# Hybrid decoder trunk: operands of the products in one aligned pool, slice-major first tiles, and the extra columns as 64-column float32 products

## The chip, the cores and the metric

The kernel runs on one NeuronCore of a Trainium2 chip. Its time is the device time of one execution in microseconds (us), and the median of three executions is compared. "PE" is the matrix engine (PEld its weight loads), DVE, ACT and POOL are the vector, scalar and GpSimd engines, and SP issues the transfers. A change of about 0.2% is what a measurement of this kernel can tell from none.

## The reference

Two layers over 512 tokens of width 1024, all in float32:

```python
for l in range(DEPTH):
    h = rms_norm(x, attn_norm[l])
    proj = h @ w_in[l]            # gates, MLA columns, RWKV columns, conv columns
    o_a = mla_branch(...) @ mla_w_o[l]
    o_b, v_first = rwkv7_branch(...)      # a scan over time, in 8 chunks of 64 in the kernel
    o_b = o_b @ rwkv_w_o[l]
    o_c = short_conv_branch(conv_cols, conv_w[l]) @ conv_w_o[l]
    merged = g[:, :, 0] * o_a + g[:, :, 1] * o_b + g[:, :, 2] * o_c
    x = x + merged @ w_out[l]
    h2 = rms_norm(x, mlp_norm[l])
    x = x + jnp.square(jax.nn.relu(h2 @ w_up[l])) @ w_down[l]
```

The "extra columns" are 32 columns of `w_in` (the shared rotary key) and, in the second layer, 32 columns of `rwkv_v1`. They are needed as one tile of 64 rows, `ext`.

## The kernel before, in words

Activations lie feature-major: 128 features on the partitions, 512 tokens along a row, 8 such slices for the width. A large product is made with three products of a reduced float32 type (fp32r): each operand is split into `hi` and a remainder `lo`, and hi·hi, hi·lo and lo·hi are added up in PSUM (`gemm_steps`, lines 269, 271 and 273). An output tile of 128 features over 8 slices is thus 24 products of 128x512. The weights stream in blocks of 512 columns: a transfer into `raw`, a cast by ACT into `hi` (line 243) and a subtraction by DVE into `lo` (line 244), in the order in which `_blocks` packs them. `xg` holds the split, gain-scaled input; its norm `rstd` is multiplied in when a tile leaves PSUM.

PE's order is the order in which the code is written. The work of a layer is: the first tiles (RWKV columns and the extra columns), the RWKV stage with its chains of small float32 products, attention, the merge of the three branches with `w_out`, and the MLP in four quarters (8 tiles up, 8 tiles down). The generator `independent` (`others`) yields the products that nothing waits for, and `fill(n)` puts n of them between small products that have to wait; the table `FC` holds the n of each place. DVE, ACT, POOL and SP instructions are ordered by the compiler's scheduler, each engine's queue then runs in order.

Places that the change touches:

- Start of a layer: five tiles one after the other (`rwkv_gemm` for "g", "g", "a", "b", "a"); the fourth (layer 0) is the extra columns, padded with zeros to 128. Tile by tile, the first needs all 8 slices of `xg` before it is finished.
- The am stage (lines 668 to 717): DVE and ACT make `ar` and `bk`, and PE multiplies them at line 714 after `fill(FC["am"])`, for j = 0 and 1.
- `chunk_inputs` (lines 840 to 843): 8 products of 64x64, four in one quarter of the array, then four in the other.
- The merge (lines 1164 to 1176): for each m a spilled `z` is read back, multiplied with the branch, added to `mg[m]` (line 1170) and split into `ar` (line 1174) and `mix` (line 1175).
- Tile buffers: one SBUF pool `sb`, which lays its tags out one behind the other in the order of their first use. In `prep` a buffer is 520 words (2080 bytes of a partition) and in `mg` 514 words (2056 bytes), so that their buffers start at many different places of a 2048-byte raster. In the built program `hi`, `lo` and `xg` lie below 79 KB, and start at byte 1120 of the raster; `mix` starts at 640 and `ar` at 672, both above 140 KB; `prep` starts at 1120, 1152, 1184 and so on, `mg` at 672, 704, 736 and so on.

Of the kernel before, what the change touches and what calls it, by code (L numbers as in the profile page):

```python
# [32 lines left out]
C = 64  # L33
# [7 lines left out]
FC = {"ss": 9, "pk": 16, "am": 42, "tri0": 6, "tri1": 10, "join0": 22, "join1": 9, "join2": 8, "in1": 9, "py": 2,  # L41
# [16 lines left out]
def _blocks(inp, l):  # L58
# [3 lines left out]
    for t in RW_ORDER[:3]:  # L62
        out.append(_cols(w_in[:, r0 + t * P:r0 + (t + 1) * P]))
    ex = np.zeros((D, P), w_in.dtype)
    ex[:, 0:32] = w_in[:, a0 + 640:a0 + 672]
    if l > 0:
        ex[:, 32:64] = inp["rwkv_v1"][l - 1]
    out.append(_cols(ex))
    for t in RW_ORDER[3:]:
        out.append(_cols(w_in[:, r0 + t * P:r0 + (t + 1) * P]))  # L70
# [96 lines left out]
def trunk(tc, w, wkv, wq, xin, pos, pp, sm, rg, out, sizes):  # L167
# [4 lines left out]
    const = es.enter_context(tc.tile_pool(name="const", bufs=1))  # L172
    sb = es.enter_context(tc.tile_pool(name="sb", bufs=1))
# [4 lines left out]
    BUFS = {"xg": 16, "mix": 8, "prep": 10, "am": 1, "ar": 4, "inv": 9, "tok": 2, "raw": 3, "hl": 4, "z": 2,  # L178
            "mg": 11, "col": 7, "g": 2, "a": 2, "b": 2, "c": 2}
# [66 lines left out]

    def load_kq(src):
# [4 lines left out]
        hi = tl("prep", (P, 520), F32R)[:, 0:n]  # L252
        lo = tl("kql", (P, WW), F32R, bufs=4)[:, 0:n]
# [33 lines left out]
    def split(tag, src, scale=None, tag_lo=None):  # L287
# [10 lines left out]
        return hi, lo  # L298

# [126 lines left out]
    def rounded(dst, src):  # L426
        ti = tl("prep", (P, 520), I32)[:, 0:NR]
# [64 lines left out]
    for l in range(NL):  # L492
        pr, dv, rgl = ppt[l], drv[l], rgt[l]
        sl = tl("sm", (P, 3 * RW), bufs=1)
        nc.sync.dma_start(out=sl, in_=sm[l])
# [30 lines left out]
        pgs = []  # L526
        at = 2 if l else 3
# [8 lines left out]
        V.tensor_tensor(out=ext[0:64, 1:T + 1], in0=pgs[0][0:64], in1=rstd[0:64], op=ALU.mult)  # L536
        rwkv_cols(RW_ORDER[3], pgs[1])
        for t in RW_ORDER[4:]:
# [24 lines left out]
        def independent():  # L563
# [6 lines left out]
            for j in range(2):  # L570
                cols = []
                for _ in range(3):
                    pg = pt("g")
                    yield from gemm_steps(pg, None, xg)
                    cols.append(evacuated(pg, tl("mg", (P, T + 2))[:, 0:T]))
                    if len(cols) == 2:
                        u = tl("mg", (P, T + 2))
# [89 lines left out]
        for j in range(2):  # L667
# [5 lines left out]
            V.tensor_scalar(out=k2, in0=a_, scalar1=dv[:, 6 + j:7 + j], scalar2=dv[:, 8 + j:9 + j],  # L673
                            op0=ALU.mult, op1=ALU.add)
            V.tensor_tensor(out=k2, in0=k2, in1=kt[j], op=ALU.mult)
            V.tensor_scalar(out=a_, in0=a_, scalar1=-0.5, scalar2=-0.5, op0=ALU.mult, op1=ALU.add)
            eW = tl("prep", (P, 8, C + 1))
# [4 lines left out]
            V.tensor_copy(eC[:, j, :], eW[:, :, C])  # L682

            ex = tl("prep").rearrange("p (b h c) -> p b h c", b=NB, h=2)
            V.tensor_copy(ex, rs16v[:, :, j, :].unsqueeze(3).to_broadcast([P, NB, 2, C]))
# [20 lines left out]
            fill(FC["am"])  # L706
# [115 lines left out]
        def chunk_inputs(b):  # L822
# [17 lines left out]
            for p in range(2):  # L840
                for h, hs in enumerate(hss):
# [43 lines left out]
        def code_split(t):  # L885

            gcol = pcol("kva", t) if t < 2 else pcol("qa", t - 2)
            hi = tl("prep", (P, 520), F32R)[:, 0:T]
# [357 lines left out]
```

## Time and profile before

| | |
|---|---|
| runs shown | 1633.64, 1634.8, 1635.77 us; median 1634.8 |
| profiled execution | 1636.34 us |
| its span, first to last instruction | 1634.6 us |
| granted PE clock, mean | 0.998 |
| busy | PE 99%, PE weight loads 80%, DVE 62%, ACT 40%, POOL 11% |
| products (PE instructions) | 8126 |

How to read it: a product's row shows its duration from first word in to last word out, about 390 ns, but the next product starts while it drains. The distance from start to start, not the duration, is what a product costs the queue of PE; so the busy share of PE is high even where it is slowed. A float32 product that isn't a transpose appears as two records. In a windows view a row is: stretch, its length, busy time and count for each engine asked for, granted PE clock, share of the transfer engines, GB/s. In a timeline a row is start, duration, engine, line, operation, and in brackets the idle time before it with what ended it.

### The profile page before, as it was taken

Reading aid. Unit: us, or ns where it says so; the run is one execution under the profiler, and the core shown is the slowest. Engines: PE = TensorE matmul, PEld = TensorE weight load, DVE = VectorE, ACT = ScalarE, POOL = GpSimd, SP = SyncE. Lnnn points to the kernel's source line nnn. Section 1 sums busy time; section 2 is a strip of 40 time slices with the busy share of each in tenths; the row PEclk is TensorE's granted clock in tenths of the full one; section 3 lists DMA queues with packets and bytes.
Section 4 is the critical chain, followed back from the end, with each engine's and each line's share of the span. In section 5 each row is a group of like instructions: output and inputs, shape, how many; then the busy total and the mean of one; then the engine's idle time right before and its main releaser. Section 6 shows DMA issues by size and latency. Waiting matters only on the chain.

```text
span 1634.6 us, 22593 instructions
## 1 busy us (share of the span) xinstructions
PE 1617.3 (99%) x8126; PEld 1306.0 (80%) x8126; DVE 1016.8 (62%) x1988; ACT 659.3 (40%) x1457; POOL 185.8 (11%) x192
## 2 busy tenths in 40 slices
PE   8999999999999999999999999999999999999998
PEld 7878778877788888888887887887777888888887
DVE  7789577676754444544567886686766544444453
ACT  5332556454443232424333335654534433323241
POOL 1212024102100000000022121251120000000000
PEclk9999999999999999999999999999999999999999
DMA  5323322214323333333432243222143333333333
GB/s 163 95 73 108 110 66 80 82 46 129 123 91 97 97 97 95 95 95 97 141 98 78 79 127 92 63 72 73 51 146 113 92 95 97 97 97 96 93 96 103
DMA packets 85072, 156.79 MB, mean 96 GB/s; under 512 B 10080, under 2 KB 12384, under 8 KB 84448
## 3 DMA queue, kind: packets, MB, share of 16 engines
q1 hardware_dynamic: 84960, 155.35, 32.3%
q8 instruction: 64, 1.05, 0.3%
q14 instruction: 48, 0.39, 0.1%
HBM read 146.40 MB, written 8.91 MB: 95 GB/s over the span
## 4 chain that ended last, share of the span: by engine, by line
PE 93%; DVE 3%; DMA 2%; issue 1%; ACT 0%; SPq 0%; POOL 0%; DVEq 0%; ACTq 0%
PE pg L271 15%; PE pg L269 15%; PE pg L273 15%; PE pa L273 4%; PE pa L271 4%; PE pa L269 4%; PE pb L273 4%; PE pb L271 4%; PE pb L269 4%; PE pc L271 4%; PE pc L273 4%; PE pc L269 4%; PE pa L1115 2%; DMA z<-z_spill 1%; PE pc L1141 1%; DVE lo L244 1%
## 5 line engine op out<-in xcount | busy, mean ns | idle before, releaser
L243 ACT CAST hi<-raw 128x512 fp32r<-128x512 f32 (+1 forms) x499 | 307.1, 618 | 629.2 <-PE pg L271 255.6
L244 DVE TENSOR_TENSOR lo<-raw,hi 128x512 fp32r<-128x512 f32 (+1 forms) x499 | 358.2, 718 | 244.6 <-ACT hi L243 239.1
L269 PE MATMUL pg<-xg,hi 128*128 128x512 f32 x784 | 312.3, 398 | 2.9 <-ACT xg L296 2.2
L271 PE MATMUL pg<-xg,hi 128*128 128x512 f32 x784 | 313.8, 400 | 0.3 <-DVE xg L297 0.3
L273 PE MATMUL pg<-xg,lo 128*128 128x512 f32 x784 | 310.0, 395 | 0.0
L269 PEld LDWEIGHTS pg<-xg,hi 128*128 128x128 f32 x784 | 147.9, 189 | 39.3 <-issue 4.7
L271 PEld LDWEIGHTS pg<-xg,hi 128*128 128x128 f32 x784 | 148.0, 189 | 34.2 <-issue 5.8
L273 PEld LDWEIGHTS pg<-xg,lo 128*128 128x128 f32 x784 | 147.8, 189 | 31.6 <-issue 2.3
L303 POOL TENSOR_TENSOR t<-t,mhalf 128x4 f32<-128x4 f32 (+1 forms) x26 | 48.9, 1882 | 560.8 <-DVE t L314 536.7
L269 PE MATMUL pg<-ar,hi 128*128 128x512 f32 x192 | 75.7, 394 | 0.1
L273 PE MATMUL pg<-ar,lo 128*128 128x512 f32 x192 | 75.5, 393 | 0.0
L273 PE MATMUL pa<-xg,lo 128*128 128x512 f32 x160 | 62.6, 391 | 0.0
L269 PE MATMUL pa<-xg,hi 128*128 128x512 f32 x160 | 62.3, 390 | 0.0
L271 PE MATMUL pa<-xg,hi 128*128 128x512 f32 x160 | 62.3, 389 | 0.0
L271 PE MATMUL pg<-mix,hi 128*128 128x512 f32 x144 | 57.5, 399 | 1.3 <-DVE mix L1175 1.3
L273 PE MATMUL pb<-xg,lo 128*128 128x512 f32 x144 | 56.2, 390 | 0.0
L269 PE MATMUL pb<-xg,hi 128*128 128x512 f32 x144 | 56.1, 390 | 0.0
L271 PE MATMUL pb<-xg,hi 128*128 128x512 f32 x144 | 56.0, 389 | 0.0
L1119 ACT ACTIVATE inv<-pa,t 128x128 f32<-128x128 f32 (+3 forms) x64 | 33.7, 527 | 46.2 <-DVE t L1117 45.7
L271 PE MATMUL pg<-prep,hi 128*128 128x512 f32 x128 | 50.5, 394 | 0.0
L269 PE MATMUL pc<-xg,hi 128*128 128x512 f32 x128 | 50.0, 390 | 0.0
L273 PE MATMUL pc<-xg,lo 128*128 128x512 f32 x128 | 49.8, 389 | 0.0
(385 smaller groups left out, 3197.7 us busy)
## 6 DMA issues: line engine op xcount, KB each, us to landing
raw<-in_w_dram SPq DMA_DIRECT2D x493, 256.0 KB, 2.6
z_spill<-z SPq DMA_DIRECT2D x16, 256.0 KB, 3.1
z<-z_spill SPq DMA_DIRECT2D x16, 256.0 KB, 2.9
raw<-in_wq_dram SPq DMA_DIRECT2D x12, 192.0 KB, 2.3
am<-in_x_dram SPq DMA_DIRECT2D x8, 256.0 KB, 6.1
raw<-in_wkv_dram SPq DMA_DIRECT2D x8, 256.0 KB, 2.7
am<-in_x_dram SPq DMA_DIRECT2D x2, 1024.0 KB, 6.1
x_spill<-am SPq DMA_DIRECT2D x8, 256.0 KB, 2.9
```

Source lines behind the costliest of these rows:

```text
L243: A.copy(hi[:, c], raw[:, c])
L244: V.tensor_tensor(out=lo[:, c], in0=raw[:, c], in1=hi[:, c], op=ALU.subtract)
L269: mm(dst, hi[:, c0:c0 + P], ah, start=(k == 0), stop=False)
L271: mm(dst, hi[:, c0:c0 + P], al, start=False, stop=False)
L273: mm(dst, lo[:, c0:c0 + P], ah, start=False, stop=(k == n - 1))
L303: G.tensor_tensor(out=y, in0=v, in1=mhalf.to_broadcast([P, n]), op=ALU.pow)
L1115: mm(psc[:, 0:n], qT[hf][h // 2][0:HD, h % 2, b * P:n], kT[hf][h // 2][0:HD, h % 2, 0:n], start=True, stop=False)
L1119: A.activation(out=pe[:, 0:n], in_=psc[:, 0:n], func=AF.Exp, bias=nm[:, h:h + 1], accum_out=rsum[:, h:h + 1])
L1141: mm(po[halves[i], f], Vm[hf][kb // 2][:, kb % 2, 2 * f + i], pT[2 * f + i][:, kb * P:(kb + 1) * P], start=(kb == 0), stop=(kb == b))
```

## The change

- A second pool `sbl` is laid out before `sb` and takes `hi`, `lo`, `xg`, `prep`, `mix`, `ar` and `mg`. `prep` and `mg` lose their padding (the padded `eW` and `u` go to `kql`, 520 words). In the built program every buffer of the seven tags now starts at byte 1120 of the 2048-byte raster, between 7 KB and 129 KB (the last buffer of `mg` ends at 132,192 bytes). `raw` gets a fourth buffer.
- The first four tiles are made slice by slice: for each of the 8 slices one weight block holds the 128 columns of all four tiles, and 12 products follow, 3 into each of four PSUM banks. `pack` orders the weights so, and the first transfers alternate between x and weight blocks.
- The extra columns leave the fp32r path: their weights are 64 columns wide, multiplied by the gains on DVE (`weights_by`), and 8 plain float32 products of 64 columns go alternately into the lower and upper half of one PSUM tile; the halves are added after an ACT copy.
- In the am stage two DVE operations, a DVE copy and a small copy per j go to ACT; the fill is 50 for j = 0 and 40 for j = 1 (42 for both before).
- `chunk_inputs` alternates between the two quarters of the array.
- In the merge `z` comes into `inv` (9 buffers; `z` has 2), and the split is written through `places`; the last two are scheduled with priority. The MLP's splits use `places` too.

```diff
-FC = {... "am": 42, ...
+FC = {... "am": (50, 40), ...
...
+    for k in range(KD):
+        out.append(np.concatenate([f[k * P:(k + 1) * P] for f in first], axis=1))
     out.append(_cols(ex))
-    for t in RW_ORDER[3:]:
+    for t in RW_ORDER[4:]:
...
+    sbl = es.enter_context(tc.tile_pool(name="sbl", bufs=1))
     sb = es.enter_context(tc.tile_pool(name="sb", bufs=1))
...
-        if tag in ("prep", "mg") and tuple(shape) == (P, T):
-            return sb.tile([P, 520 if tag == "prep" else T + 2], dt, tag=tag, name=f"{tag}_{cnt[0]}", bufs=BUFS[tag])[:, 0:T]
-        return sb.tile(list(shape), dt, tag=tag, name=f"{tag}_{cnt[0]}", bufs=bufs or BUFS[tag])
+        pool = sbl if tag in ("hi", "lo", "xg", "prep", "mix", "ar", "mg") else sb
+        return pool.tile(list(shape), dt, tag=tag, name=f"{tag}_{cnt[0]}", bufs=bufs or BUFS[tag])
...
+    def weights_by(gains):
+
+        i, off = wpos
+        wpos[0], wpos[1] = i + 1, off + WW * P
+        raw = tl("raw", (P, WW))
+        nc.sync.dma_start(out=raw, in_=w[off:off + WW * P].rearrange("(p n) -> p n", p=P))
+        wx = tl("inv").rearrange("p (k n) -> p k n", n=C)
+        V.tensor_tensor(out=wx, in0=raw.rearrange("p (k n) -> p k n", n=C), in1=gains.unsqueeze(2).to_broadcast([P, KD, C]),
+                        op=ALU.mult)
+        return wx
...
+    def places(m, tag):
+
+        if tag is None:
+            return tuple(tl("mix" if m < 4 else "prep", (P, T), F32R) for _ in range(2))
+        if m < 4:
+            both = tl("ar", (P, 2, T), F32R)
+            return both[:, 0], both[:, 1]
+        return tuple(tl(tag, (P, T), F32R) for _ in range(2))
...
-        if k in (0, 3):
-            ahead.append(load_weights(2))
-    ahead += [load_weights(2), load_weights()]
+        if k < 4:
+            ahead.append(load_weights(2 if k < 2 else 1))
...
-        for i, pst in enumerate(("g", "g", "a", "b", "a")):
-            pgs.append(rwkv_gemm(pst, normed_steps if i == at else None))
-            if i == at:
+        pgs = [pt(pst) for pst in ("g", "g", "a", "b")]
+        for k, (ah, al) in enumerate(xg):
+            hi, lo = weights()
+            for t, pg in enumerate(pgs):
+                c = slice(t * P, (t + 1) * P)
+                mm(pg, hi[:, c], ah, start=(k == 0), stop=False)
+                mm(pg, hi[:, c], al, start=False, stop=False)
+                mm(pg, lo[:, c], ah, start=False, stop=(k == KD - 1))
+        for _ in normed_steps:
+            pass
...
+        wx = weights_by(pr[:, PC["attn"]:PC["attn"] + 8])
+        pe = pt("a")
+        for k in range(KD):
+            i = k % 2
+            mm(pe[halves[i]], wx[:, k], xt[:, k], start=(k < 2), stop=(k >= KD - 2))
+        pgs.append(pt("b"))
+        for i, _ in enumerate(gemm_steps(pgs[4], None, xg)):
+            if i == 8:
                 normed_spread()
...
+        odd = tl("inv")
+        A.copy(odd[0:64], pe[64:128])
...
-            V.tensor_scalar(out=k2, in0=a_, scalar1=dv[:, 6 + j:7 + j], scalar2=dv[:, 8 + j:9 + j],
-                            op0=ALU.mult, op1=ALU.add)
+            A.activation(out=k2, in_=a_, func=AF.Identity, scale=dv[:, 6 + j:7 + j], bias=dv[:, 8 + j:9 + j])
...
-            for p in range(2):
-                for h, hs in enumerate(hss):
+            for h, hs in enumerate(hss):
+                for p in range(2):
                     mm(prs[p][halves[1 - p], hs], AM[halves[p], h, b, p, halves[1 - p]], uvs[p][halves[p], hs],
...
-            z = tl("z")
+            z = tl("inv")
             nc.sync.dma_start(out=z, in_=zd[l][:, m * T:(m + 1) * T])
             run(branch_steps(z, wb, oa, 0, P, z))
-            (V if m > 5 else G).tensor_tensor(out=mg[m], in0=mg[m], in1=z, op=ALU.add)
...
+            merged.append(places(m, "mix"))
+            with tc.high_priority() if m > 5 else nullcontext():
+                (V if m > 5 else G).tensor_tensor(out=mg[m], in0=mg[m], in1=z, op=ALU.add)
+                split_into(merged[m], mg[m])
```

PE's queue at the very start, before; `xg_138` and `xg_139` are hi and lo of slice 0, `xg_142` and `xg_143` of slice 1, `pg_323` is the first tile:

```order
L269 MATMUL pg_323<-xg_138,hi_99 128x512
L271 MATMUL pg_323<-xg_139,hi_99 128x512
L273 MATMUL pg_323<-xg_138,lo_100 128x512
L269 MATMUL pg_323<-xg_142,hi_99 128x512
L271 MATMUL pg_323<-xg_143,hi_99 128x512
```

The same place in the change; `pg_321`, `pg_322`, `pa_323` and `pb_324` are the four tiles:

```order
L556 MATMUL pg_321<-xg_138,hi_102 128x512
L557 MATMUL pg_321<-xg_139,hi_102 128x512
L558 MATMUL pg_321<-xg_138,lo_103 128x512
L556 MATMUL pg_322<-xg_138,hi_102 128x512
L557 MATMUL pg_322<-xg_139,hi_102 128x512
...
L558 MATMUL pb_324<-xg_138,lo_103 128x512
L556 MATMUL pg_321<-xg_142,hi_112 128x512
```

Slice 1 is used by the fourth product before, and by the thirteenth now.

DVE's queue in the am stage of layer 0, before, up to the last operand of line 714 (`ar_812`):

```order
L673 TENSOR_SCALAR prep_914<-prep_756,drv_265 128x512
L678 MEMSET prep_918 128x8
L696 TENSOR_TENSOR ar_811<-prep_809,prep_766 128x4x128
L702 TENSOR_TENSOR ar_812<-prep_762,prep_760 128x4x2x64
L685 COPY prep_923<-t_140_740 128x512
L244 TENSOR_TENSOR lo_935<-raw_933,hi_934 128x512
L675 TENSOR_TENSOR prep_914<-prep_914,mix_574 128x512
L676 TENSOR_SCALAR prep_756<-prep_756 128x512
L682 COPY eC_708<-prep_918 128x8
L700 TENSOR_TENSOR prep_809<-prep_809,prep_748 128x512
...
L701 TENSOR_TENSOR ar_812<-prep_809,prep_760 128x4x128
```

The same stretch in the change (`ar_791` is the operand):

```order
L720 TENSOR_TENSOR prep_910<-prep_910,mix_553 128x512
L741 TENSOR_TENSOR ar_790<-prep_788,kql_745 128x4x128
L747 TENSOR_TENSOR ar_791<-prep_741,prep_739 128x4x2x64
L247 TENSOR_TENSOR lo_870<-raw_868,hi_869 128x512
L745 TENSOR_TENSOR prep_788<-prep_788,prep_727 128x512
L777 SCALAR_TENSOR_TENSOR prep_741<-mix_535,pp_81,prep_741 128x512
L593 TENSOR_TENSOR col_826<-pg_775,rstd_320 128x512
L746 TENSOR_TENSOR ar_791<-prep_788,prep_739 128x4x128
```

The instructions of lines 673, 676, 682 and 685 are gone from DVE's queue, for both j (they stand in ACT's).

SP's queue in the merge of layer 0, before; `z_4401` and so on are the read-backs, the `raw` rows between them weight blocks:

```order
L1168 DMA z_4401<-z_spill_93 128x512
L242 DMA raw_4528<-in_w_dram 128x512
L242 DMA raw_4554<-in_w_dram 128x512
L1168 DMA z_4428<-z_spill_93 128x512
L242 DMA raw_4581<-in_w_dram 128x512
L1168 DMA z_4454<-z_spill_93 128x512
L242 DMA raw_4611<-in_w_dram 128x512
```

In the change the read-backs go into `inv`:

```order
L1213 DMA inv_4380<-z_spill_96 128x512
L1213 DMA inv_4406<-z_spill_96 128x512
L1213 DMA inv_4432<-z_spill_96 128x512
L1213 DMA inv_4458<-z_spill_96 128x512
L1213 DMA inv_4484<-z_spill_96 128x512
L245 DMA raw_4532<-in_w_dram 128x512
L1213 DMA inv_4511<-z_spill_96 128x512
```

Five read-backs now stand in a row ahead of the weight block `raw_4532`, which is that of m = 6.

More of the change, by code (lines that the diff above doesn't have):

```diff
@@ L61, in _blocks @@
     out = []
-    for t in RW_ORDER[:3]:
-        out.append(_cols(w_in[:, r0 + t * P:r0 + (t + 1) * P]))
-    ex = np.zeros((D, P), w_in.dtype)
+    first = [w_in[:, r0 + t * P:r0 + (t + 1) * P] for t in RW_ORDER[:3]]
+    ex = np.zeros((D, C), w_in.dtype)
     ex[:, 0:32] = w_in[:, a0 + 640:a0 + 672]
@@ L176, in trunk @@
     dram = es.enter_context(tc.tile_pool(name="dram", bufs=1, space=bass.MemoryType.DRAM))
-    BUFS = {"xg": 16, "mix": 8, "prep": 10, "am": 1, "ar": 4, "inv": 9, "tok": 2, "raw": 3, "hl": 4, "z": 2,
-            "mg": 11, "col": 7, "g": 2, "a": 2, "b": 2, "c": 2}
+    BUFS = {"xg": 16, "mix": 8, "prep": 10, "am": 1, "ar": 4, "inv": 9, "tok": 2, "raw": 4, "hl": 4, "z": 2,
+            "mg": 11, "col": 7, "kql": 4, "g": 2, "a": 2, "b": 2, "c": 2}
     cnt = [0]
@@ L298, in split, with split_into @@
         return hi, lo
+    def places(m, tag):
[5 more added lines that the diff above has]
+        return tuple(tl(tag, (P, T), F32R) for _ in range(2))
+    def split_into(hl, src):
+        A.copy(hl[0], src)
+        V.tensor_tensor(out=hl[1], in0=src, in1=hl[0], op=ALU.subtract)
     def rsqrt(v, n):
@@ L426, in rounded @@
     def rounded(dst, src):
-        ti = tl("prep", (P, 520), I32)[:, 0:NR]
+        ti = tl("prep", (P, T), I32)[:, 0:NR]
         V.tensor_copy(ti, src)
@@ L524, in rwkv_cols @@
             mixed[t] = m_
-        pgs = []
-        at = 2 if l else 3
-        for i, pst in enumerate(("g", "g", "a", "b", "a")):
-            pgs.append(rwkv_gemm(pst, normed_steps if i == at else None))
-            if i == at:
+        pgs = [pt(pst) for pst in ("g", "g", "a", "b")]
[8 more added lines that the diff above has]
+            pass
+        sl = tl("sm", (P, 3 * RW), bufs=1)
+        nc.sync.dma_start(out=sl, in_=sm[l])
+        halves = (slice(0, C), slice(C, P))
+        wx = weights_by(pr[:, PC["attn"]:PC["attn"] + 8])
[6 more added lines that the diff above has]
+            if i == 8:
                 normed_spread()
@@ L533, in trunk @@
             rwkv_cols(t, pgs.pop(0))
+        odd = tl("inv")
+        A.copy(odd[0:64], pe[64:128])
         ext = tl("ext", (P, T + 1), bufs=1)
         V.memset(ext[0:64, 0:1], 0.0)
-        V.tensor_tensor(out=ext[0:64, 1:T + 1], in0=pgs[0][0:64], in1=rstd[0:64], op=ALU.mult)
-        rwkv_cols(RW_ORDER[3], pgs[1])
-        for t in RW_ORDER[4:]:
+        V.tensor_tensor(out=ext[0:64, 1:T + 1], in0=pe[0:64], in1=odd[0:64], op=ALU.add)
+        V.tensor_tensor(out=ext[0:64, 1:T + 1], in0=ext[0:64, 1:T + 1], in1=rstd[0:64], op=ALU.mult)
+        rwkv_cols(RW_ORDER[3], pgs[0])
+        rwkv_cols(RW_ORDER[4], pgs[1])
+        for t in RW_ORDER[5:]:
             rwkv_cols(t, rwkv_gemm())
@@ L704, in trunk @@
             BK.append(bk)
-            fill(FC["am"])
+            fill(FC["am"][j])
             for bb in range(2):
@@ L1204, in trunk @@
                 V.tensor_tensor(out=rl, in0=pu, in1=rl, op=ALU.mult)
-                if q % 2 == 0:
-                    us.append(split("mix", rl, tag_lo="prep"))
-                else:
-                    if m % 2 == 0:
-                        uh = tl("ar", (P, 2, T), F32R)
-                    lo = tl("mg", (P, T), F32R)
-                    A.copy(uh[:, m % 2], rl)
-                    V.tensor_tensor(out=lo, in0=rl, in1=uh[:, m % 2], op=ALU.subtract)
-                    us.append((uh[:, m % 2], lo))
+                us.append(places(m, "mg") if q % 2 else places(m, None))
+                split_into(us[m], rl)
             for m in range(8):
```

31 lines of the change are left out of this document (12 added, 19 removed).

## The prediction

> **What bounds the kernel now.** I read the page's first part and the chain of waits, then looked in windows and timelines for what the queue of PE really costs.
>
> ```profile
> PE 1617.3 (99%) x8126; PEld 1306.0 (80%) x8126; DVE 1016.8 (62%) x1988; ACT 659.3 (40%) x1457; POOL 185.8 (11%) x192
> ...
> PE 93%; DVE 3%; DMA 2%; issue 1%; ACT 0%; SPq 0%; POOL 0%; DVEq 0%; ACTq 0%
> ```
>
> PE is busy 99% of the span and carries 93% of the chain that ended last. Only 17.3 us (1634.6 - 1617.3) are visible idle time, so a gain must come from fewer or cheaper products, or from those idle places. Whether a product is cheap shows in the distance between starts. The MLP is best for this: nothing interrupts it, and each half quarter is 8 tiles of 24 products, 192 in all. Two halves up and two halves down of the first layer, as windows from the first start of one to that of the next, with the rows that open them:
>
> ```profile
> 509.92 0.40 PE L269 MATMUL pg<-mix,hi 128*128 128x512 f32 x1
> ...
> 554.40 0.40 PE L269 MATMUL pg<-xg,hi 128*128 128x512 f32 x1
> ...
> 597.96 0.40 PE L269 MATMUL pg<-ar,hi 128*128 128x512 f32 x1
> ...
> 642.48 0.40 PE L269 MATMUL pg<-xg,hi 128*128 128x512 f32 x1
> ```
>
> The down half that reads `mix` and `prep` takes 554.40 - 509.92 = 44.48 us, 231.7 ns per product; the one that reads `ar` and `mg` 642.48 - 597.96 = 44.52 us, 231.9 ns. The up half between them, which reads `xg`, takes 597.96 - 554.40 = 43.56 us, 226.9 ns. These are the same instructions with the same weights' buffers, at the same clock; they differ in the tiles that stream. The up half is not the freer of the two for ACT and DVE, which also make the next activations there. The starts of single products show how it differs:
>
> ```profile
> 560.56 0.39 PE L269 MATMUL pa<-xg,hi 128*128 128x512 f32 x1
> 560.79 0.39 PE L271 MATMUL pa<-xg,hi 128*128 128x512 f32 x1
> 561.01 0.39 PE L273 MATMUL pa<-xg,lo 128*128 128x512 f32 x1
> 561.24 0.39 PE L269 MATMUL pa<-xg,hi 128*128 128x512 f32 x1
> ```
>
> ```profile
> 512.69 0.39 PE L269 MATMUL pg<-mix,hi 128*128 128x512 f32 x1
> 512.92 0.40 PE L271 MATMUL pg<-prep,hi 128*128 128x512 f32 x1
> 513.16 0.40 PE L273 MATMUL pg<-mix,lo 128*128 128x512 f32 x1
> ```
>
> The first run keeps an even beat (three products in 0.68 us), the second goes 0.23, 0.24 and has longer products. The groups of the MLP, and a window on the branch products of the merge, which stream `prep` alone:
>
> ```profile
> L273 PE MATMUL pa<-xg,lo 128*128 128x512 f32 x160 | 62.6, 391 | 0.0
> ...
> L271 PE MATMUL pa<-prep,hi 128*128 128x512 f32 x64 | 25.2, 394 | 0.0
> L273 PE MATMUL pa<-mix,lo 128*128 128x512 f32 x64 | 25.2, 394 | 0.0
> ...
> 394.80:418.60 23.80, 23.80 (x103) 1.00 0.47 143
> ```
>
> All buffers of `xg` share their start in the 2048-byte raster (1120) with the weights. The slow ones start elsewhere: `mix` at 640, `ar` at 672, `prep` and `mg` at a different place for each buffer. `prep` lies below 128 KB and `mix` above, yet a chain of `prep` alone is slow too (23.80 us / 103 = 231 ns), so a mere limit at 128 KB does not explain it.
>
> **The change part by part.**
>
> 1. Operands in one aligned pool. After it, all streams of fp32r products start at byte 1120, as `xg` does now. I take it that they then keep its beat: 231.8 - 226.9 = 4.9 ns per product. Eight down halves are 1536 products, 7.5 us. The merge (96 products on `prep`) and `w_out` (192 on `ar` and `mix`), in two layers, are 576 more: 2.8 us as an estimate, since they read the same kinds of tiles. Sum **-10.3 us**; bounds: 0 (placement is not the cause) and -11 (a little from the `oc` and `ob` chains, which interrupt `xg`).
>
> A rule speaks against this part. The Trainium skill (SBUF — State Buffer, Who interferes with whom) says that "PE and ACT never wait on anyone", and gives each of PE's two reads a port of its own; by it the place of a tile would not matter, the term would be nothing and the sum 10.3 us smaller. The rows above do not agree with it as it stands: the same products differ by 4.9 ns with the tiles that they stream.
>
> 2. Extra columns. Removed are 24 products per layer at 227 ns, 5.4 us. Added are 8 float32 products of 64 columns and 512 words. The nearest rows are the attention's values, float32 products in alternating halves of the array with 128 words, and a full-width float32 product of 512 words:
>
> ```profile
> 341.67:343.13 1.46, 1.46 (x24) 1.29 (x24) 1.00 0.00 0
> ...
> 343.13 1.12 PE L1115 MATMUL pa<-ar,ar 96*128 96x512 f32 x2
> 344.09 0.22 PE L1116 MATMUL pa<-cmask,identb 128*128 128x128 bf16 x1
> ```
>
> The window holds 24 records of line 1141 in 1.46 us, 61 ns each with entry and exit, for 128 words. For 512 words that is at most 243 ns, and 16 records (8 products, two each) cost 3.9 us. Were the halves not to work side by side, a record would cost what line 1115 does, (344.09 - 343.13) / 2 = 0.48 us, and 16 would cost 7.7 us. I take the first, since the halves are used in the same way: **-3.0 us** for two layers; bounds -3.6 and +4.6. The one weight block less, the DVE product for `wx` and the ACT copy `odd` are hidden by PE.
>
> 3. `chunk_inputs` in alternating quarters. Before:
>
> ```profile
> 176.24:177.04 0.80, 0.80 (x16) 0.80 (x16) 1.00 0.96 192
> ```
>
> 16 records of line 842 in 0.80 us, 50 ns each, though some overlap already where the quarters change. Line 714 alternates between two halves now, with 128 words: its 32 records run from 83.39 us (row below) to 85.38 us, 62 ns each, so 31 ns for half the words. 16 x 31 = 0.50 us: 0.30 us less, eight times, **-2.4 us**; bounds 0 and -2.8.
>
> 4. Slice-major start. Before, slice 1 comes late, and the queue stands:
>
> ```profile
> 5.52 0.80 PE L269 MATMUL pg<-xg,hi 128*128 128x512 f32 x1
> ...
> 9.35 0.50 PE L269 MATMUL pg<-xg,hi 128*128 128x512 f32 x1 [2.15 <-ACT xg L296]
> ...
> 33.77 0.38 PE L323 MATMUL pc<-ident,tok 128*128 128x128 f32 x2
> ...
> 0.00:20.00 20.00, 16.08 (x58) 12.78 (x59) 15.84 (x72) 12.63 (x23) 2.07 (x25) 0.91 0.70 211
> ```
>
> The first 96 products end at 33.77 us, with the 8 small ones of the norm (about 0.8 us) among them. After it, 12 products of slice 0 fill the time from 5.52 us, the 84 of slices 1 to 7 begin at about 9.7 us (slice 1 still lands when it did, and its block of weights needs a cast of about 0.4 us), and last 84 x 0.227 = 19.1 us: 28.8 us, 29.6 with the norm. That is **-4.0 us**. It needs 4 MB by the last slice at 26 us; at the 211 GB/s of the first 20 us they land in 20 us. Bounds: 0, if the blocks come late, and -5. The second layer's start shows no wait for slices, so nothing is gained there.
>
> 5. The am stage, in both layers:
>
> ```profile
> 81.16 0.39 PE L269 MATMUL pg<-xg,hi 128*128 128x512 f32 x1
> ...
> 83.39 0.37 PE L714 MATMUL pa<-ar,ar 64*128 64x128 f32 x1 [1.84 <-DVE ar L701]
> ...
> 85.38 1.12 PE L734 MATMUL pc<-prep,bones 128*128 128x512 f32 x2
> 85.94 0.79 PE L271 MATMUL pg<-xg,hi 128*128 128x512 f32 x1
> ...
> 891.01 0.39 PE L269 MATMUL pg<-xg,hi 128*128 128x512 f32 x1
> ...
> 893.50 0.37 PE L714 MATMUL pa<-ar,ar 64*128 64x128 f32 x1 [2.11 <-DVE prep L678]
> ...
> 893.50:897.66 4.16, 4.16 (x35) 0.59 0.43 126
> ...
> L673 DVE TENSOR_SCALAR prep<-prep,drv 128x512 f32<-128x512 f32 x4 | 2.1, 530 | 0.0
> L676 DVE TENSOR_SCALAR prep<-prep 128x512 f32<-128x512 f32 x4 | 1.7, 422 | 0.0
> ```
>
> PE stands for 2.23 - 0.23 = 2.0 us and 2.49 - 0.23 = 2.3 us. Eight more fill products put 1.8 us ahead of line 714, and DVE loses at least 2 x (0.53 + 0.42) = 1.9 us from the chain that is late: **-4.3 us**. ACT, 40% busy, takes the work; were it late instead, the gain would fall to the 1.8 us of fill. For j = 1 the fill loses 0.45 us, less than DVE gains. After the second stop the clock is 0.59 for 4.16 us; the same products take 85.94 - 83.39 = about 2.6 us in layer 0. Without the stop this **-1.6 us** goes too.
>
> 6. The merge. `w_out` waits for the last splits:
>
> ```profile
> 392.39 1.90 PE pc L1141 x32
> ...
> 396.17 0.40 PE L269 MATMUL pg<-prep,hi 128*128 128x512 f32 x1
> ...
> 422.88 0.39 PE L269 MATMUL pg<-ar,hi 128*128 128x512 f32 x1
> 424.33 0.50 PE L271 MATMUL pg<-mix,hi 128*128 128x512 f32 x1 [1.06 <-DVE mix L1175]
> ...
> 1235.71 0.50 PE L271 MATMUL pg<-mix,hi 128*128 128x512 f32 x1 [0.27 <-DVE mix L1175]
> ```
>
> Read-backs five deep and the priority should take **-1.3 us** of this. But the read-backs are now queued on SP ahead of the block of m = 6, and the third waits for attention's last reads: if that were late, PE would wait for weights instead. Attention's last values end at about 394.3 us. The branches start at 396.17 and go 12 products each, so m = 6 starts 72 x 0.231 = 16.6 us later, at about 413: I see no wait. Bounds +2 and -2.
>
> Sum: -10.3 - 3.0 - 2.4 - 4.0 - 4.3 - 1.6 - 1.3 = **-26.9 us** against the profiled execution's span of 1634.6. That execution's own time is 1636.34, 1.5 us over the median of the runs; I take the difference from the median, 1634.8: **1608 us**.
>
> **The rivals.** A: placement isn't what makes the beat; the first term is zero and the time 1618. For it speaks that in attention, between small products, `xg` too loses its beat, from the same buffers, so that what came before a product counts as well. Against it: in the MLP the beat comes back each time that `xg` does. B: the 64-column halves run one after the other: +2.3 instead of -1.5 us per layer with the upper price, 1616. Against it: the row of line 1141. C, the slower side: the new addresses make the beat uneven for all products, `xg` included, since weights and streams now lie close together. By the program 3600 products on `xg` (226.9 ns now) and 2400 others (231.8) are left; the other parts gain 16.6 us, so a beat above (3600 x 226.9 + 2400 x 231.8 + 16600) / 6000 = 231.6 ns is slower than before. At 234 ns it would be 14 us more, 1649. Against it: `xg` keeps its beat in all of its sixteen buffers.
>
> **How the numbers follow.** The forecast 65%, A 18%, B 7%, C 4%; 6% for parts 4 to 6 giving only half while the first holds (about 1613). The forecast's own range is 1601 to 1613; to leave out no more than 2 in 10 the range is 1601 to 1619, which takes in A. About 0.2% (3.3 us) is what a measurement can tell from no change. Faster by more: all cases but C and a mixture of A and B with half gains, 0.92; same 0.04; slower 0.04.
>
> **What would show it.** Part 1: the down halves at about 43.6 us like the up halves; if they stay at 44.5, A holds. Part 2: the eight products in under 4.2 us per layer; 7 or more is B. Part 3: 16 records in 0.5 us. Part 4: the norm's products before 30.5 us. Part 5: no idle time ahead of line 759's products and a full clock near 890 us. Part 6: no row of `w_out` with a wait. The prediction is wrong if the up halves slow down, or if a new wait of over 1 us stands on PE.

## The result, and the profile after

The changed kernel takes 1606.93 us (median of four runs, 1606.35 to 1607.23), the kernel before in the same session 1635.28 us: a ratio of 0.9827, with a 95% interval of 0.981 to 0.9844. The forecast was 1608 us within 1601 to 1619. The total was met to about 1 us, but not every part of the sum: one brought next to nothing, and others brought more than they were given.

The page of the changed kernel, its busy times and the shares of the chain that ended last:

```profile
span 1604.9 us, 22533 instructions
...
PE 1593.0 (99%) x8110; PEld 1295.2 (81%) x8110; DVE 1016.3 (63%) x1971; ACT 664.1 (41%) x1470; POOL 185.8 (12%) x192
...
PE 98%; DVE 1%; DMA 0%; ACT 0%; issue 0%; SPq 0%; DVEq 0%; ACTq 0%
```

PE's visible idle time fell from 17.3 us to 11.9 (1604.9 - 1593.0), and its share of the chain rose from 93% to 98%. PE's busy share is 99% in both kernels, although its products became cheaper: the busy share did not show that there was something to gain; the distance between starts did.

The windows view of PE, with the stretch, its length, PE's busy time and the count of products, the granted clock, the share of the transfer engines and GB/s. First three halves of the first layer's MLP in the changed kernel (down on `mix` and `prep`, up on `xg`, down on `ar` and `mg`), then the branches of the merge and `w_out` in layer 0:

```profile
497.53:541.05 43.52, 43.52 (x194) 1.00 0.34 97
541.05:584.57 43.52, 43.52 (x194) 1.00 0.34 97
584.57:628.09 43.52, 43.52 (x194) 1.00 0.34 97
...
386.81:408.58 21.77, 21.77 (x97) 1.00 0.44 151
408.58:452.10 43.52, 43.52 (x193) 1.00 0.36 103
```

The same two stretches of the merge in the kernel before:

```profile
396.17:418.64 22.47, 22.47 (x98) 1.00 0.50 152
418.64:464.51 45.87, 44.81 (x194) 1.00 0.34 104
```

All halves now take 43.52 us, 192 x 226.67 ns, but for the first up half of a layer, in which the norm's products stand; the down halves took 44.48 and 44.52. The branches (21.77 us / 96) and `w_out` keep the same beat, and the slow products at the seam of two halves are gone too: that is why the up halves fell from 43.56 to 43.52 us.

The timeline of PE at the start and at the am stages of the changed kernel (start, duration, engine, line, operation, and in brackets idle time with what ended it):

```profile
9.04 0.39 PE L556 MATMUL pg<-xg,hi 128*128 128x512 f32 x1
...
28.08 0.94 PE L336 MATMUL pc<-ones,inv 128*128 128x1 f32 x8
...
28.95 3.65 PE L569 MATMUL pa<-am,inv 128*64 128x512 f32 x16
32.54 0.50 PE L283 MATMUL pb<-xg,hi 128*128 128x512 f32 x1
...
76.76 0.37 PE L759 MATMUL pa<-ar,ar 64*128 64x128 f32 x1
...
874.83 0.37 PE L759 MATMUL pa<-ar,ar 64*128 64x128 f32 x1
```

The twelve products of slice 0 are followed at 9.04 us by those of slice 1 without a wait, and the first 96 products and the norm's eight end at 28.95 us (33.77 before). The eight float32 products of the extra columns take 32.54 - 28.95 = 3.59 us. Line 759 starts without a wait in both layers (1.84 and 2.11 us before).

Where the 29.7 us between the two spans went, by the starts of the same instructions in both traces, with 0.2267 us for each fp32r product that stands on the other side of the mark:

| part | forecast | in the traces | how read |
|---|---|---|---|
| 1 operands in one raster | -10.3 | -11.8 | MLP -4.1 in each layer; merge and `w_out` together -5.6, less the waits of part 6 |
| 2 extra columns | -3.0 | -3.7 | 2 x (3.59 - 24 x 0.2267) |
| 3 `chunk_inputs` | -2.4 | about -0.4 | the run that undoes it, below |
| 4 slice-major start | -4.0 | -4.8 | 28.95 - 33.77, first layer only |
| 5 am stage and clock | -5.9 | -5.6 | 1.9 and 2.1 less ahead of line 759, 1.6 less behind it in the second layer |
| 6 merge | -1.3 | -2.0 | waits of 1.2, 0.3 and 0.4 gone |
| not foreseen: a wait in attention | 0 | -0.8 | 0.4 in each layer, ahead of line 1160 |

The parts add up to -29.1 of the 29.7; the remaining 0.6 us has no row. How the merge's gain is split between parts 1 and 6 depends on which is taken first (see part 6 below).

### The profile page after: what moved, and what is told of

It reads as the page before. It is cut to its first block, busy times and chain, and to the rows that moved or that the text cites. A ratio compares the mean times of both kernels' runs of the same rounds, so it can differ in the third digit from the quotient of the medians.

```text
span 1604.9 us, 22533 instructions
## 1 busy us (share of the span) xinstructions
PE 1593.0 (99%) x8110; PEld 1295.2 (81%) x8110; DVE 1016.3 (63%) x1971; ACT 664.1 (41%) x1470; POOL 185.8 (12%) x192
## 4 chain that ended last, share of the span: by engine, by line
PE 98%; DVE 1%; DMA 0%; ACT 0%; issue 0%; SPq 0%; DVEq 0%; ACTq 0%
PE pg L283 16%; PE pg L285 16%; PE pg L287 16%; PE pb L283 4%; PE pb L285 4%; PE pb L287 4%; PE pa L287 4%; PE pa L285 4%; PE pc L285 4%; PE pc L287 4%; PE pc L283 4%; PE pa L283 4%; PE pa L1160 2%; PE pc L1186 1%; PE pb L1174 1%; PE pa L968 1%
## 5 line engine op out<-in xcount | busy, mean ns | idle before, releaser
L283 PE MATMUL pg<-xg,hi 128*128 128x512 f32 x736 | 292.7, 398 | 0.7 <-DVE z L600 0.7
L285 PE MATMUL pg<-xg,hi 128*128 128x512 f32 x736 | 292.7, 398 | 0.0
L287 PE MATMUL pg<-xg,lo 128*128 128x512 f32 x736 | 289.9, 394 | 0.0
L283 PEld LDWEIGHTS pg<-xg,hi 128*128 128x128 f32 x736 | 138.4, 188 | 34.6 <-issue 4.3
L285 PEld LDWEIGHTS pg<-xg,hi 128*128 128x128 f32 x736 | 138.5, 188 | 30.9 <-issue 5.2
L287 PEld LDWEIGHTS pg<-xg,lo 128*128 128x128 f32 x736 | 138.4, 188 | 28.6 <-issue 1.9
L283 PE MATMUL pg<-mix,hi 128*128 128x512 f32 x128 | 50.6, 395 | 0.0
L287 PE MATMUL pg<-mix,lo 128*128 128x512 f32 x128 | 50.3, 393 | 0.0
L287 PE MATMUL pa<-xg,lo 128*128 128x512 f32 x128 | 50.0, 391 | 0.0
L283 PE MATMUL pc<-xg,hi 128*128 128x512 f32 x128 | 50.0, 391 | 0.0
L285 PE MATMUL pa<-xg,hi 128*128 128x512 f32 x128 | 49.8, 389 | 0.0
L283 PE MATMUL pa<-xg,hi 128*128 128x512 f32 x128 | 49.8, 389 | 0.0
L285 PE MATMUL pc<-xg,hi 128*128 128x512 f32 x128 | 49.8, 389 | 0.0
L654 POOL TENSOR_TENSOR mg<-mg,z 128x512 f32<-128x512 f32 x16 | 23.7, 1482 | 186.0 <-DVE z L607 144.9
```

The lines of the kernel that those rows point to most:

```text
L283: mm(dst, hi[:, c0:c0 + P], ah, start=(k == 0), stop=False)
L285: mm(dst, hi[:, c0:c0 + P], al, start=False, stop=False)
L287: mm(dst, lo[:, c0:c0 + P], ah, start=False, stop=(k == n - 1))
L654: G.tensor_tensor(out=mg[m], in0=mg[m], in1=z, op=ALU.add)
```

## The experiments: what makes the beat

Five kernels ask what it is about a tile's place that costs the 5 ns. The first takes the kernel before and changes places; two padded tiles (`eW` and `u`) also move to `kql`, since `prep` and `mg` lose their padding:

```diff
+    sbx = es.enter_context(tc.tile_pool(name="sbx", bufs=1))   # behind sb
-        if tag in ("prep", "mg") and tuple(shape) == (P, T):
-            return sb.tile([P, 520 if tag == "prep" else T + 2], ...)[:, 0:T]
+        pool = sbx if tag in ("sm", "col", "ext", "kql") else sb
```

> The kernel before with one thing changed: prep and mg lose their padding, and the tiles of odd size (sm, col, ext, kql) go into a pool behind the others, so that hi, lo, xg, prep, mix, ar and mg all start at byte 1120 of the 2048-byte raster, but prep, mix, ar and mg stay high, at 101 to 181 KB. Theory P (the place in the raster decides): the down halves of the MLP go from 44.5 to 43.5 us, w_out and the branches to 226.7 ns per product; with 2112 products x about 5 ns that is -10 to -12 us, about 1624. Theory L (the low addresses decide): down halves stay at 44.5, time within 2 us of 1635.

Measured: 1628.22 us against 1636.6 in the same session, ratio 0.9947 (0.9932 to 0.9961). Its first MLP halves, down and up, in the windows view:

```profile
510.00:553.52 43.52, 43.52 (x193) 1.00 0.32 98
553.52:597.04 43.52, 43.52 (x193) 1.00 0.33 98
```

The beat is that of the changed kernel, with the tiles still at 101 to 181 KB: theory P holds, and the low addresses are not needed for the beat. The time missed its expectation by 4 us; longer waits took some of the gain back. The waits of PE in this kernel (total, times, longest):

```profile
PE pa L714 <- DVE ar L701: 4.7, 2, 2.9
PE pg L269 <- ACT xg L296: 2.6, 1, 2.6
...
PE pg L269 <- DVE z L561: 0.8, 2, 0.4
```

and in the kernel before:

```profile
PE pg L269 <- ACT xg L296: 2.2, 1, 2.2
PE pa L714 <- DVE prep L678: 2.1, 1, 2.1
PE pa L714 <- DVE ar L701: 1.8, 1, 1.8
```

Line 714 waits 4.7 us instead of 3.9, the start 2.6 instead of 2.2, and a wait of 0.8 us on line 561 is new: 2.0 us of the 4.2 that are missing. Another 1.6 us are the session's (the kernel before took 1636.6 us in it, and 1635 was the base of the expectation).

The second goes the other way, from the changed kernel:

```diff
+        pad = {"prep": 8, "mg": 8}.get(tag, 0)     # words
+        if pad:
+            return pool.tile([P, T + pad], dt, tag=tag, ...)[:, 0:T]
```

> The changed kernel, with prep and mg padded by 32 bytes again (raw back to three buffers to make room): all seven tags stay below 133 KB, prep and mg start at a different place for each buffer, mix and ar all at 1440. Theory P: down halves of the MLP near 44.3 us (half of the streams of each are padded ones), the branches near 231 ns per product, but w_out, which reads ar and mix alone, stays near 43.5 us; time about 1607 + 8 x 0.8 + 2 x 0.45 = 1614. Theory L: down halves stay at 43.5 us, time 1607.

Measured: 1615.09 us, 0.987 of the kernel before (0.9854 to 0.9887). A down half, an up half, and `w_out`:

```profile
498.64:542.86 44.22, 44.22 (x193) 1.00 0.35 95
542.86:586.41 43.55, 43.55 (x194) 1.00 0.34 98
...
409.23:453.19 43.96, 43.96 (x193) 1.00 0.36 100
```

The down halves are slow again, below 133 KB. But `w_out` was expected to keep 43.5 us and took 43.96, 229.0 ns per product, though all its streams start at one place, 1440. Only its weights start elsewhere, at 1120, 320 bytes away (64 beyond 256). So it is not enough that neighbouring streams agree with one another. The next run asks just that:

```diff
+    # 32 bytes of space ahead of lo and again ahead of prep:
+    # hi 1120, lo and xg 1152, prep, mix, ar and mg 1184
```

> The changed kernel with two spaces of 32 bytes: hi starts at byte 1120, lo and xg at 1152, prep, mix, ar and mg at 1184 (raw three buffers). If only the streams of neighbouring products must share a place, both kinds of halves stay at 43.5 us, with some 10 slow products more where a half changes over, and the time is 1607 to 1608. If streams must share their place with the weights, the halves go to 44.5 us and the time to about 1607 + 6000 x 5 ns = 1637.

Measured: 1633.85 us (one run), nearly the whole gain lost. A down half and an up half:

```profile
503.95:548.32 44.37, 44.37 (x193) 1.00 0.34 96
548.32:593.11 44.79, 44.79 (x193) 1.00 0.34 93
```

Now the up halves are slow too, on `xg`, whose sixteen buffers agree with one another and with `lo`, but stand 32 bytes from `hi`: 44.79 us, 233.3 ns per product. Streams must share their place with the weights, and it is not enough that one product's own two tiles agree: the third of each three products here streams `xg` against `lo`, which agree, and the distance from it to the next start is 230.7 ns all the same (235.8 and 233.4 for the other two).

How coarse the raster is, two runs tell. In one each buffer of `mix` stands 256 bytes further than the last, and each of `mg` 64:

```diff
+        pad = {"mix": 64, "mg": 16}.get(tag, 0)    # words
```

> The changed kernel with each buffer of mix 256 bytes further in the raster than the one before it, and each of mg 64 bytes (raw three buffers, z one, to make room). It asks how coarse the raster is. If places need only agree in 64 bytes, all down halves stay at 43.5 us. If in 256 bytes, the even quarters (mix, prep) stay at 43.5 and the odd ones (ar, mg) go towards 44.3. If in 512 bytes or more, both go to about 44.0 to 44.5 us, and the time is some 1613.

In the other the streams stand 128, 288 and 352 bytes from the weights:

```diff
+    # 128 bytes of space ahead of xg, 160 ahead of prep, 64 ahead of ar:
+    # hi and lo 1120, xg 1248, prep and mix 1408, ar and mg 1472
```

> The changed kernel with the weights (hi, lo) at byte 1120 and three other distances of the streams from them: xg 128 bytes further, prep and mix 288 (32 beyond a multiple of 256), ar and mg 352 (96 beyond it); raw three buffers. If weights and streams need to agree in 128 bytes, the up halves of the MLP (xg) keep 43.5 us and the down halves go to 44 to 44.8. If in 256 bytes, all halves are slow and the time is near that of the run with three places, 1634 us. If some distance is better than none, one kind of half falls below 43.5 us; I expect none.

The down halves with the steps of 256 bytes (on `mix` and `prep`) and of 64 (on `ar` and `mg`):

```profile
501.14:544.66 43.52, 43.52 (x193) 1.00 0.34 97
...
588.18:632.37 44.19, 44.19 (x193) 1.00 0.33 96
```

and with the three distances, down on `mix` and `prep` (288 bytes, 32 beyond 256), up on `xg` (128), down on `ar` and `mg` (352, 96 beyond 256), and the next half up on `xg` (128 again):

```profile
504.21:549.01 44.80, 44.80 (x194) 1.00 0.30 93
549.01:593.62 44.61, 44.61 (x193) 1.00 0.34 95
593.62:638.42 44.80, 44.80 (x193) 1.00 0.33 93
638.42:683.22 44.80, 44.80 (x193) 1.00 0.32 95
```

The steps of 256 bytes cost nothing, those of 64 do (44.19 us; the kernel with the steps takes 1616.34 us, one run), and a distance of 128 does (44.61 and 44.80 us in the two up halves). The raster is 256 bytes: where all weights and streams of a stretch agree in it, a product costs 226.67 ns. At the distances that were run it costs 2 to 7 ns more in the mean of a half: 229.0 ns at 64 bytes (`w_out` in the second kernel), 233.3 at 32 and at 96, and 232.3 or 233.3 at 128. The two values at 128 show that the distance alone does not fix the cost. Nor is the slow beat even: in `w_out` at 64 bytes the distances of three successive starts are 231.8, 226.1 and 229.1 ns on average, over and over. None of the distances was better than agreement. With all streams off, this kernel takes 1637.35 us (one run), 30 us more than the changed one and as much as the kernel before.

One rival is left: that a stream must stand at a certain place of the 256 bytes, whatever the weights do. Two runs speak against it. In `w_out` the streams stand at 1440 in the second kernel and at 1184 in the one with three places, which is the same place in 256 bytes, and `hi` stands at 1120 in both. Only `lo` is 32 bytes further in the latter, and `w_out` takes 44.37 us there instead of 43.96. So the place of the weights counts too. But in every run `hi` starts at byte 1120: whether weights and streams could share any other place as well was not run. What causes the raster, no run shows; only the rule is shown.

## The experiments: the other parts, undone one at a time

The extra columns in one half of the array:

```diff
-            mm(pe[halves[i]], wx[:, k], xt[:, k], start=(k < 2), stop=(k >= KD - 2))
+            mm(pe[halves[0]], wx[:, k], xt[:, k], start=(k == 0), stop=(k == KD - 1))
```

> The changed kernel with all eight products of the extra columns in the lower half of the PSUM tile, added up there, without the ACT copy and the DVE addition. If the two halves work side by side in the changed kernel, a record now takes its full 0.43 to 0.48 us instead of 0.22, the 16 records 6.9 to 7.7 us instead of 3.6, and the time is 1607 + 2 x 3.7 = 1614. If the halves don't matter, nothing changes.

Measured: 1613.99 us. The sixteen records in this kernel:

```profile
29.78 7.08 PE L568 MATMUL pa<-am,inv 128*64 128x512 f32 x16
```

7.08 us instead of 3.65: the halves do work side by side, and rival B is priced, 3.5 us a layer. Against the 5.44 us of the 24 products removed, one half alone would have been a loss.

The start, tile by tile again:

```diff
-        for k, (ah, al) in enumerate(xg):        # slice by slice
+        pgs = [rwkv_gemm(pst) for pst in ("g", "g", "a", "b")]
```

with the weights packed and loaded in the old order.

> The changed kernel with the first four tiles made one after the other again, weights packed and loaded in the old order. If the slice-major order itself saves what the two traces differ by, the first 96 products and the norm end some 4.8 us later in the first layer and nothing changes in the second: 1611 to 1612 us. If the rest of the path (the norm, DVE's work up to line 759) sets the end of that stage, part of it is hidden there: +1 to +3 us.

Measured: 1610.73 us, 0.9839 of the kernel before (0.9824 to 0.9853), 3.8 us more than the changed kernel. The old wait is back:

```profile
8.78 0.50 PE L283 MATMUL pg<-xg,hi 128*128 128x512 f32 x1 [1.82 <-ACT xg L310]
```

It stands between its two expectations. Slice 1 came at 8.78 us in this run and at 9.35 in the kernel before, so that line 759 of the first layer starts 4.1 us later than in the changed kernel, not 4.8; by the end of each layer's chunk stage some 0.4 us of this is made up again, since PE waits less there. The second layer's start has no such wait.

`chunk_inputs` in the old order:

```diff
-            for h, hs in enumerate(hss):
-                for p in range(2):
+            for p in range(2):
+                for h, hs in enumerate(hss):
```

> The changed kernel with the eight products of chunk_inputs in the old order, four in one quarter of the array, then four in the other. The 16 records take 0.74 us from first to last start again instead of 0.46. If this is on the path in all eight chunks, it costs 8 x 0.28 = 2.2 us, 1609. If PE waits for ACT and DVE behind the first and the third chunk of a layer anyway, only the others lose: +0.5 to +1.1 us, 1607.5 to 1608.

Measured: 1607.14 us (1606.85 to 1607.21), 0.2 us more than the changed kernel. Its waits of PE in the chunk stages:

```profile
PE pa L228 <- DVE st L989: 1.1, 2, 0.5
...
PE pa L968 <- ACT rv L891: 0.5, 2, 0.3
PE pa L968 <- DVE rr L954: 0.2, 1, 0.2
```

The same waits in the changed kernel:

```profile
PE pa L228 <- DVE st L989: 1.6, 2, 0.8
...
PE pa L968 <- ACT rv L891: 1.1, 2, 0.5
PE pa L968 <- DVE rr L954: 1.0, 2, 0.5
```

And the first of them in the timeline of the changed kernel:

```profile
169.12 0.68 PE L887 MATMUL pb<-uv,am 64*64 64x64 f32 x16
170.34 0.65 PE L968 MATMUL pa<-rv,prep 64*64 64x64 f32 x8 [0.54 <-ACT rv L891]
```

The records do run closer (0.46 us from the first start to the last instead of 0.74, 8 x 0.28 = 2.2 us), but the waits behind them grow from 1.8 to 3.7 us in total. PE finishes its products sooner and then stands for ACT and DVE. By the starts, the chunk stages of the two layers are only some 0.4 us shorter with the new order.

Of the am stage and of the merge, each layer undoes another half. For am:

```diff
-            fill(FC["am"][j])
+            fill((FC["am"] if l else (42, 42))[j])
+            # layer 1: the four operations on DVE again
```

> The changed kernel with one half of the am stage's change undone in each layer: in the first the fill is 42 and 42 again (ACT keeps the moved operations), in the second the operations go back to DVE (the fill stays 50 and 40). In the changed kernel the last operand is written at 74.99 us and line 759 starts at 76.76, so there is slack of 1.8 us in the first layer, and 2.4 in the second. If the prediction's sum is right that it needs both, undoing one brings back a wait of about 2 us in each layer, 1611. If either would have been enough, the waits stay under 0.5 us and the time within 1 us of 1607.

Measured: 1609.16 us. In the first layer line 766, which is 759 there, has no wait with the old fill; in the second, with the operations on DVE, it has:

```profile
75.42 0.37 PE L766 MATMUL pa<-ar,ar 64*128 64x128 f32 x1
...
877.50 0.37 PE L766 MATMUL pa<-ar,ar 64*128 64x128 f32 x1 [1.07 <-DVE ar L753]
```

So moving the four operations was enough by itself in the first layer, and the longer fill alone was not in the second: 1.07 us of wait are left. Neither theory had that: undoing either was to bring back about 2 us, or neither was. The first layer as a whole still ends 1.5 us later by the starts, in small waits at its start, on `z` and in attention, none of them at line 766.

For the merge:

```diff
-            z = tl("inv")
+            z = tl("inv" if l else "z")
-            with tc.high_priority() if m > 5 else nullcontext():
+            with tc.high_priority() if m > 5 and l == 0 else nullcontext():
```

> The changed kernel with one half of the merge's change undone in each layer: in the first the read-backs go into the two buffers of z again (the priority stays), in the second the last two splits have no priority (the read-backs stay in inv). If the deeper read-backs remove the waits of w_out, the first layer shows again about 1.2 us ahead of the first product on mix, the second nothing; if the priority does it, the second shows 0.3 and 0.4 us and the first nothing. Time 1607 to 1609.

Measured: 1608.36 us. With the read-backs in `z`, the first layer waits again, in the branches and at `w_out`:

```profile
406.23 0.47 PE L283 MATMUL pg<-prep,hi 128*128 128x512 f32 x1 [0.41 <-DVE z L607]
...
414.43 0.50 PE L285 MATMUL pg<-mix,hi 128*128 128x512 f32 x1 [0.68 <-DVE mix L325]
```

Branches and `w_out` take 67.28 us there instead of 65.29. Without the priority the second layer has no wait there and takes 65.31 us, as in the changed kernel. So the depth of the read-backs is needed in the first layer, where the priority alone does not remove the waits; the priority is not needed in the second.

## Two attempts at a faster version

The changed kernel waits 3.7 us in the chunk stages, while the am fill ends well after its operands. The last `ar` in the first layer:

```profile
74.31 0.68 DVE L743 TENSOR_TENSOR ar<-mix,kql 128x512 f32<-128x512 f32 x1
```

It is ready at 74.99 us, and line 759 starts at 76.76. So products were moved from the one place to the other:

```diff
-FC = {... "am": (50, 40), ...
+FC = {... "am": (44, 26), ...
+                fill(3)                                  # behind the first chunk's inputs
-                fill(FC["py"])
+                fill(FC["py"] + (3 if c == 4 else 0))
-                fill(FC["pr"])
+                fill(FC["pr"] + {3: 4, 5: 1}.get(c, 0))
+        # col: 2304 bytes a buffer; raw: three buffers
```

> An attempt at a faster version of the changed kernel. The am fill falls from 50 and 40 to 44 and 26, since the operands of line 759 are ready 1.8 to over 3.8 us early; 11 of these products go to the places of the chunk stage where PE waits now (3 behind the first chunk's inputs, 4 ahead of the fourth's and 1 ahead of the sixth's, 3 into the fifth chunk), and the tags col get 2304 bytes a buffer, so that the lo of code_split agrees with the other operands in 256 bytes (raw three buffers). If the waits of 0.7, 1.0, 0.6 and 0.2 us a layer are waits that any product can fill, 2 x 2.5 us are saved at most, and 0.5 us by the place: 1602. If the chain of ACT and DVE is only pushed back by it, the time stays at 1607; if am's new fill is too short, waits of up to 2 us come back there.

Measured: 1610.26 us (1609.89 to 1610.55), slower than the changed kernel. The chunk stages did become 1.2 us shorter each, for equal products, but new waits stand elsewhere:

```profile
PE pg L285 <- DVE z L602: 2.0, 4, 0.6
...
PE pg L287 <- DVE prep L1194: 1.4, 2, 0.7
PE pa L761 <- DVE ar L748: 0.9, 1, 0.9
```

The second attempt kept `raw`, `col` and the first am fill:

```diff
-FC = {... "am": (50, 40), ...
+FC = {... "am": (50, 31), ...
+                fill(3)
+                fill(FC["py"] + (2 if c == 4 else 0))
+                fill(FC["pr"] + (4 if c == 3 else 0))
```

> A second attempt: raw and col as in the changed kernel, the first am fill stays 50, the second falls from 40 to 31; the 9 products go to the chunk stage (3 behind the first chunk's inputs, 4 ahead of the fourth's, 2 into the fifth chunk). In the first attempt the chunk stage became 1.25 us shorter in each layer, but PE lost 1.4 and 2.4 us ahead of it (the am stage, and finished tiles that DVE had not yet taken out of PSUM) and 1.0 us in the branches. If those losses came from the short am fill and the three raw buffers, they are gone and the time is 1607 - 2 x 1.2 = 1604.5. If every shift of the filling products makes them meet DVE's other work, it stays at 1607 or above.

Measured: 1607.88 us (1607.86 to 1608.07), 0.983 of the kernel before (0.9816 to 0.9843); its profiled execution is 1.4 us longer than that of the changed kernel (spans 1606.3 and 1604.9). The chunk stage of the first layer, in windows, in the changed kernel and in this one:

```profile
169.12:208.34 39.22, 37.40 (x300) 1.00 0.29 86
```

```profile
169.12:209.02 39.90, 39.90 (x309) 1.00 0.31 96
```

Nine products more fit into 0.68 us more, where they cost 9 x 0.227 = 2.04 us elsewhere: 1.4 us gained a layer, and PE has no idle time left there. But ahead of it, in PE's timeline:

```profile
149.81 0.39 PE L287 MATMUL pg<-xg,lo 128*128 128x512 f32 x1
151.88 0.47 PE L283 MATMUL pg<-xg,hi 128*128 128x512 f32 x1 [1.69 <-DVE z L600]
```

and in DVE's:

```profile
147.43 3.58 DVE L834 STREAM_TRANSPOSE prep<-inv 32x256 f32<-32x256 f32 x8 [0.59 <-ACT inv L828]
151.04 0.69 DVE L600 TENSOR_TENSOR z<-pg,rstd 128x512 f32<-128x512 f32 x1
```

Nine filling products fewer ahead of this place mean that another product of the list falls here: it now opens a tile whose PSUM buffer is still held by a finished one, and DVE, which has to take that out (line 600), is in the middle of eight transposes. 1.7 us are lost in the first layer and 2.2 in the second, more than was gained. The changed kernel remains the fastest of those run; the one with the old order of `chunk_inputs` (1607.14 us) cannot be told from it.

## Why the prediction was right, and where it was not

**Part 1 held in its size and its mechanism, with two corrections.** The down halves fell to the up halves' time, and the run in place shows that it is the tiles' place in the raster. The sum was 1.5 us too small: the seams between `xg` and the other tiles cost some ten slow products each, and these went too; and -4.9 ns per product was taken from a whole up half with its slow beginning, where the free beat against 231.8 is 5.1. The prediction spoke of streams that start at one place; that the weights must share it was among what it noted of `xg` ("share their start ... with the weights"), but was not made the rule. The runs with three places and three distances show it, and those with steps that 256 bytes of agreement are enough, not 2048. The window that it read as `prep` alone opens with six products on `mix` and `col`; the 96 on `prep` behind them took 22.47 us, 234 ns each with some short waits, so the reading stands. Rival A (1618) falls with the run in place. What spoke for A, that `xg` too loses its beat in attention, is not settled: in the changed kernel too, a run of aligned products that follows other work starts unevenly (at 831 us the starts are 314, 235, 233, 236, 224 ns apart) and takes some ten products to settle at 227.

The rule of the Trainium skill (SBUF — State Buffer, Who interferes with whom) that was weighed there, "PE and ACT never wait on anyone", does not agree with these runs if it is read as the prediction read it, that the place of a tile does not matter: 32 bytes more in the place of the streams cost 233.3 - 226.7 = 6.6 ns a product on PE, at a granted clock of 1.00.

**Part 2 held, and rival B is refuted and priced.** 3.59 us instead of the forecast 3.9 a layer: the row that bounded it, 61 ns for 128 words, held entry and exit as well, as the prediction said of it (3.59 / 16 = 0.224 us for 512 words, 56 ns for 128).

**Part 3 failed.** The step "0.30 us less, eight times" took a shorter run of products for a shorter path. The records are shorter as forecast; but behind the first and the third of a layer's four calls PE waits for what ACT and DVE make of them, and these waits grew by nearly as much. Its lower bound, 0, named the possibility, and the rows of the waits on lines 923 and 225 in the kernel before could have shown it: a chain that PE already waits for doesn't end sooner when PE is done sooner with something else ahead of it.

**Part 4** was 0.8 us too small at its place: the products of slice 1 began at 9.04 us, not at 9.7, since slice 1 and its weights were there in time. Undone by itself it is worth 3.8 us of the 4.8, for the two reasons given there.

**Part 5** was right in its sum to 0.3 us, but not in its reason. It added the fill's 1.8 us and DVE's 1.9 as if both were needed. With both, line 759 has 1.8 us to spare in the first layer, and there the operations moved to ACT suffice alone. The granted clock behind line 759 is 1.00 in the second layer too, as forecast, where it was 0.59 behind the stop of 2.11 us; behind the 1.07 us of wait in the run that undoes a half it was 1.00 as well.

**Part 6** was too small by 0.7 us. Its 1.3 us are the two idle times that the rows show (1.06 and 0.27); by the starts these cost 1.2 and 0.4 us, and a third wait of 0.3 went too. No weights came late, as the prediction had worked out from the order on SP. The part is worth more once the beat is faster: in the first of the five kernels, with aligned tiles but the old read-backs, branches and `w_out` take 67.28 and 67.31 us in the two layers, against 68.34 and 67.82 before and 65.29 and 65.31 in the changed kernel. Taken in that order, alignment alone gives the merge 1.6 us, less than the 2.8 that part 1 put there, and the merge's own changes 4.0: with the faster beat and the old read-backs PE stands idle there for 2.2 us, not 1.4.

**Rival C** (a slow beat for all) did not come about. A slow beat for all does exist, but under another condition than C's, that weights and streams lie close together: with the streams 32 to 128 bytes off the weights in 256 bytes, the changed kernel takes 1637 us.

The errors of parts 3 and 5 (+2.0 and +0.3) and of the others (-1.5 -0.7 -0.8 -0.7 and the 0.8 in attention that no part had) partly cancel, so that meeting the total to about 1 us is in part luck. The sum, 26.9 us, came out 2.8 us below the difference of the spans, and 1.5 us below that of the medians (28.4 us): the execution profiled before was slower than its median.

## What to carry to other kernels

Read the cost of a product from the distance between starts, not from busy time, and compare stages that do the same with other tiles: a difference of 2% with nothing idle was the largest single gain here. Let weights and streams of fp32r products agree in 256 bytes of their address; padding a tile by a few words is enough to lose it. And before a chain of small products is shortened, look who waits behind it; before filling products are moved into a wait, look what else the list of filling products shifts.

## What was not expected of the hardware

That the place of a stream relative to the weights, in a raster of 256 bytes, changes the distance between products: 226.67 ns at agreement, and in the mean of a half 229.0 at 64 bytes, 233.3 at 32 and 96, and 232.3 or 233.3 at 128, the same in both layers. And that the order of small products in the quarters of the array, which shortened 16 records from 0.74 to 0.46 us, could vanish so completely in the time.
